# A down projection that streams 512 weight columns per stationary tile instead of 256

## The chip, the cores and the metric

The kernel runs on one core of a Trainium2 chip. The metric is the device time of one execution in microseconds (us); lower is better. The core has a matrix engine (PE in the profile, its weight loads PEld), a vector engine (DVE), a scalar engine (ACT), a general engine (POOL) and a queue engine (SP), which here issues weight loads. Each engine carries out its own instructions strictly in the order in which the program gives them, and waits at an instruction whose inputs or whose output buffer aren't free yet.

## The reference

One block of a diffusion model on 2048 tokens of width 1024: a gated linear attention branch and a pooling branch are mixed and added to the input, and then a mixture of experts follows. Only that last part is touched here. In it, 16 experts each choose the 256 tokens with the highest affinity to them (`top_k` over the tokens), and for each expert

```
xs = hs[idx]                                             # 256 tokens x 1024
a  = silu(xs @ w_gate_e) * (xs @ w_up_e)                 # 256 x 1024
y  = (a @ w_down_e) * wgt                                # 256 x 1024, the down projection
out = zeros.at[idx].add(y)
```

The result is scaled by a gate, added to the running activation, and every token row is normalized (`rms_norm` with `final_norm_g`). All arrays are float32.

## The kernel before, in words

**Three products for one.** To keep float32 accuracy at the matrix engine's fast rate, each operand is split into a high part in a shortened float32 format and a low part (the rest). `mm3` (L252 to L255) issues three matmuls for one product: high by high, high by low, low by high. Each has a stationary operand of 128x128 and a moving operand that streams past it.

**Weight units.** All weights come as units of 128x1024 float32 (512 KB), in one fixed list (`Units`, L60 to L108). For a unit, SP loads the raw tile `wraw` (3 buffers), ACT copies it to `whi` (L78), and DVE subtracts to get `wlo` (L85; POOL does it during the first expert, L1905). `whi` and `wlo` have 3 buffers each (the two 3s of L282): unit n+3 is written where unit n was, so its split on ACT can begin only when PE has finished with unit n.

**Items.** The order of all engines is written out by one Python loop. `Flow.item(n, mm)` (L156) does this for one piece of matrix work: it issues the matmuls of n units; then one step of the searches that are registered as `early`; then the eviction ("post") of the item before, with `flush_part`; then one step of each side generator; then the splits of as many units as the item gave back (`ahead`); and it keeps its own eviction for the next item. So DVE sees, for one item, first the splits behind that item and then, in the next item, its eviction.

**An expert** (loop at L1898) is 8 items `gate_up` (L1790; 2 units each: one tile of gate and one of up weights stationary, the 256 tokens moving, 48 matmuls of 256 columns into one bank `pA`), and then 4 items `down` (L1809; 2 units each). In a down item, `ah` and `al` (the activations, high and low) are stationary, 128 tokens at a time, and 256 columns of the down weights are moving: 2 token tiles x 8 contraction tiles x 3 = 48 matmuls. Both token tiles share one `pA` bank, 256 columns each. `LATE` (L45) gives the order: contraction tile 7, which needs the last gate_up item's activations, comes at the end. The eviction `fin` (L1823) multiplies each half by the token weights and the gate `gt2` on DVE (L1825) into `y`. Accumulator banks: `pA` has 3 buffers (L1591), `pG` 2 and `pT` 3. Between gate_up and down, and after down, `fl.flush()` issues the waiting eviction at once.

**Side work.** One step per item: `prep` (L1726) of the next expert (the one-hot tiles L1731, the gather of tokens, transposes), in the first expert also the search for the token choice of experts 2 to 15 (`topk_rest`, L1711, an `early` generator: a count on DVE, then the matmul L1719), and in the last six experts (`special`) more: after the eviction `fin_cols` (L1920) adds the old rows (L1922), `fin_late` (L1883) sums squares on ACT, `final_row` writes finished rows, and 16 generators `norm_row` (L1836), started 4 steps apart, normalize the rows of all tokens.

In the last expert's last down item (`split`) the two token tiles have a bank each, and the first tile is finished before the second begins.

Of the kernel before, what the change touches and what calls it, by code (L numbers as in the profile page):

```python
# [10 lines left out]
F32 = mybir.dt.float32  # L11
F32R = mybir.dt.float32r
BF = mybir.dt.bfloat16
I32 = mybir.dt.int32
AF = mybir.ActivationFunctionType
OP = mybir.AluOpType
# [5 lines left out]
L = 2048  # L22
LC = 256
KC = 8
T = 512
# [3 lines left out]
E = 16  # L29
# [15 lines left out]
LATE = ((0, range(4)), (1, range(4)), (0, range(4, 7)), (1, range(4, 7)), (0, (7,)), (1, (7,)))  # L45
# [184 lines left out]
def build(ctx, tc, A, out, dbg=None):  # L230
# [10 lines left out]
    def ps_a():  # L241
        return psum.tile([128, 512], F32, name="pA", bufs=2)
# [9 lines left out]
    def mm3(ps, lh, ll, rh, rl, first, last):  # L252
        PE.matmul(ps, lh, rh, start=first, stop=False)  # L253
        PE.matmul(ps, lh, rl, start=False, stop=False)  # L254
        PE.matmul(ps, ll, rh, start=False, stop=last)  # L255
# [27 lines left out]
    fl = Flow()  # L283
# [1522 lines left out]
            return fin  # L1806
        fl.item(2, mm)

    def down(j, ah, al, y, wt, cols, after, split):  # L1809
        cs = slice(j * 256, (j + 1) * 256)  # L1810

        def mm(w):
            ph = [ps_a(), ps_a()] if split else [ps_a()] * 2
            ph = [t[:, i * 256:(i + 1) * 256] for i, t in enumerate(ph)]
            for i, ks in ((0, range(KC)), (1, range(KC))) if split else LATE:
                for kc in ks:
                    wh, wl = w[kc // 4]
                    s = slice(kc % 4 * 256, (kc % 4 + 1) * 256)
                    ts = slice(i * 128, (i + 1) * 128)
                    mm3(ph[i], ah[:, kc, ts], al[:, kc, ts], wh[:, s], wl[:, s],  # L1820
                        kc == 0 and (i == 0 or split), kc == KC - 1 and (i == 1 or split))

            def fin():  # L1823
                for i in range(2):
                    V.scalar_tensor_tensor(y[i][:, cs], ph[i], wt[:, i:i + 1], gt2[:, cs],  # L1825
                                           op0=OP.mult, op1=OP.mult)
                    if cols:
                        cols(j, i)
                if after:
                    after()  # L1830
            return fin
        fl.item(2, mm)

    LASTK = 6

# [46 lines left out]

    def fin_late(j, i, e, y, acs, ss4, cs):  # L1883
        yield
        jf = mo.tile([128, L], BF, name="jf")[:, :256]
        S.activation(jf, y[i][:, cs], AF.Square, accum_out=ss4[:, i, j:j + 1])
        if e == E - 1:
            (V if j == 3 else G).tensor_mul(acs[i][:, cs], y[i][:, cs], fng[:, cs])

    res = {}  # L1890
    rest, keys = topk_rest(), keys_rest()
# [6 lines left out]
    for e in range(E):  # L1898
        special = e >= E - LASTK
        xh, xl, idx, wt = res.pop(e)  # L1900
        ah = mo.tile([128, 8, 256], F32R, name="ah", bufs=2)
        al = mo.tile([128, 8, 256], F32R, name="al", bufs=2)
        if e + 1 < E:
            fl.add(prep(e + 1, res))
        un.low2 = G if e == 0 else V  # L1905
        if e == 0:
            fl.early.append(rest)
            fl.add(chain(delay(AD), split_aff(slice(HEAD_N, E), E - HEAD_N)))
        acs = []
        if special:  # L1910
            fl.add(acc_gather(idx, acs))
        if e == E - LASTK:
            fl.add(chain(delay(2), staggered([lambda t=t: norm_row(t) for t in range(NSC)], 4)))
        for f in range(8):
            gate_up(f, xh, xl, ah, al)
        y = [mo.tile([128, D], F32, name=f"y{i}", bufs=2) for i in range(2)]

        ss4 = mo.tile([128, 2, 4], F32, name="ss4", bufs=2)

        def fin_cols(j, i, e=e, y=y, acs=acs, ss4=ss4, idx=idx):  # L1920
            cs = slice(j * 256, (j + 1) * 256)
            V.tensor_add(y[i][:, cs], y[i][:, cs], acs[i][:, cs])  # L1922
            if j < 2 or e < E - 1:
                fl.add(fin_late(j, i, e, y, acs, ss4, cs))
                return
            for _ in fin_late(j, i, e, y, acs, ss4, cs):
                pass
            if j == 3 and e == E - 1:
                for _ in final_row(i, e, y, acs, ss4, idx):
                    pass  # L1930

        def scat(e=e, y=y, idx=idx, special=special, ss4=ss4, acs=acs):
            if special and e < E - 1:
                fl.add(chain(delay(1), staggered([lambda i=i: final_row(i, e, y, acs, ss4, idx) for i in range(2)], 1)))
            elif not special:
                for i in range(2):
                    G.indirect_dma_start(out=x1_d[:, :],
                                         out_offset=bass.IndirectOffsetOnAxis(ap=idx[i][:, :1], axis=0),
                                         in_=y[i], in_offset=None, compute_op=OP.add)
        fl.flush()  # L1940
        for j in range(4):
            down(j, ah, al, y, wt, fin_cols if special else None, scat if j == 3 else None,
                 e == E - 1 and j == 3)
        fl.flush()
        if e == E - 1:
            fl.drain()
# [6 lines left out]
def host_inputs(inputs):  # L1953
    g = {k: np.ascontiguousarray(np.asarray(v)) for k, v in inputs.items()}
    c = np.ascontiguousarray
    w_in = g["w_in"][0]
    k0, v0, r0, q0, g0, p0, m0 = 0, 256, 768, 800, 1056, 1568, 2080

    def st_units(w):
        n = w.shape[1] // 128  # L1960
        return w.reshape(KC, 128, n, 128).transpose(2, 1, 0, 3).reshape(n, 128, 1024)

    def mv_units(w):
        n = w.shape[1] // 256
        return w.reshape(2, 4, 128, n, 256).transpose(3, 0, 2, 1, 4).reshape(2 * n, 128, 1024)

    rr = w_in[:, r0:r0 + 32]
    win = np.concatenate([st_units(np.concatenate([rr, rr, rr, rr], 1)), st_units(w_in[:, k0:k0 + 256]),
                          st_units(w_in[:, q0:q0 + 256]), mv_units(w_in[:, v0:v0 + 512]),
                          st_units(w_in[:, g0:g0 + 512]), st_units(w_in[:, p0:p0 + 512]),  # L1970
                          st_units(w_in[:, m0:m0 + 2048])])
    wdu = g["w_decay_up"][0].reshape(2, 16, H, 64)
    w32 = np.zeros((32, H, 128), np.float32)
    w32[0:16, :, 0:64] = wdu[0]
    w32[16:32, :, 64:128] = wdu[1]
    w32 = w32.reshape(32, 512)
    ab = g["ada_b"][0]
    vecs = np.concatenate([g["c"].reshape(8, 128), g["c_ctx"].reshape(8, 128), g["norm1_g"].reshape(8, 128),
                           ab[0:1024].reshape(8, 128), ab[1024:2048].reshape(8, 128),
                           g["b_decay"][0].reshape(2, H, 64).transpose(1, 0, 2).reshape(H, 128),  # L1980
                           g["pool_scale"].reshape(4, 128), g["gla_norm_g"].reshape(1, 128)])
    aw = g["ada_w"][0]
    ada1 = aw[:, :2048].reshape(KC, 128, 4, 512).transpose(2, 1, 0, 3)
    ada2 = aw[:, 2048:].reshape(4, 2, 128, 8, 512).transpose(3, 2, 0, 1, 4).reshape(8, 128, 4, 1024)

    def inv_counts(n):
        r = np.zeros((4, n), np.float32)
        pos = np.arange(n)
        for i, w in enumerate(WINDOWS):
            r[i] = 1.0 / (np.clip(pos + w // 2, 0, n) - np.clip(pos - w // 2, 0, n))  # L1990
        return r

    pj = np.concatenate([g["w_gla_proj"][0].reshape(4, 128, 8, 128), g["w_pool_proj"][0].reshape(4, 128, 8, 128)])
    pj = pj.transpose(2, 1, 0, 3).reshape(8, 128, 1024)
    wg = g["w_gate_e"][0].reshape(E, KC, 128, 8, 128).transpose(0, 3, 2, 1, 4).reshape(E, 8, 128, 1024)
    wu = g["w_up_e"][0].reshape(E, KC, 128, 8, 128).transpose(0, 3, 2, 1, 4).reshape(E, 8, 128, 1024)
    wdn = g["w_down_e"][0].reshape(E, 2, 4, 128, 4, 256).transpose(0, 4, 1, 3, 2, 5).reshape(E, 8, 128, 1024)
    return {
        "x": g["x"][0], "ctx": g["ctx"][0], "vecs": c(vecs), "ada1": c(ada1), "ada2": c(ada2),
        "ada_b2": c(ab[None, 2048:]), "win": c(win), "wdu": c(np.concatenate([w32] * 4)),  # L2000
        "pool_w": c(g["pool_w"][0].transpose(1, 0, 2)), "icc": inv_counts(64), "icr": inv_counts(32),
        "wpj": c(pj), "wout": c(mv_units(g["w_out"][0])),
        "w_router": c(g["w_router"][0].reshape(KC, 128, E).transpose(1, 0, 2)),
        "wg": c(wg), "wu": c(wu), "wdn": c(wdn),
        "norm2_g": g["norm2_g"].reshape(1, D), "final_norm_g": g["final_norm_g"].reshape(1, D),
    }
# [15 lines left out]
```

## Time and profile before

| | us |
|---|---|
| three runs of the kernel | 2653.22, 2662.35 (the median), 2670.72 |
| span of the profiled execution, first to last instruction | 2667.8 |
| mean granted TensorE clock in it | 0.972 |
| PE busy / DVE busy / ACT busy / POOL busy | 2517.5 / 1881.2 / 1252.5 / 659.1 |

The profiled execution's own time is its span, 2667.8 us; no other time is shown for it. It lies 5.45 us above the median of the runs and inside their spread. All stretches below are in us from the start of the span; the experts lie between 1476 and 2653. Busy times of PE are modelled (a matmul's record is longer than the distance to the next), so the distance between starts is what counts. In a timeline row the first number is the start, the second the duration, and the bracket at the end gives the idle time before it and what ended it.

### The profile page before, as it was taken

What the parts mean: (1) busy time and instruction counts of PE and PEld (TensorE: products, weight loads), DVE (VectorE), ACT (ScalarE), POOL (GpSimd) and SP (SyncE); (2) the same over time, 40 slices, a digit from 0 to 9 for tenths busy, and PEclk for the clock granted to TensorE, in tenths of its full rate; (3) what the DMA queues carried; (4) which work ended last, traced back from release to release, by engine and by line L of the source; (5) the groups of instructions that cost most, each with busy time, mean ns of one, the idle gap of its engine ahead of it and who ended that gap; (6) DMA issues with size and microseconds to landing.
All of it is one profiled execution on the core that took longest, in us unless ns stands there. A gap on an engine that the chain in (4) does not pass through costs nothing. (4 is left out here: it accounts for less than half of the span.)

```text
span 2667.8 us, 44973 instructions
## 1 busy us (share of the span) xinstructions
PE 2517.5 (94%) x17575; PEld 2295.5 (86%) x17575; DVE 1881.2 (71%) x3049; ACT 1252.5 (47%) x2128; POOL 659.1 (25%) x607
## 2 busy tenths in 40 slices
PE   7999999999998989999996899999999999999997
PEld 4878887887887768897886789999999999999997
DVE  6676668478368767767676866666666667778775
ACT  5454444344453345455553334444444445555553
POOL 0032157055225202131312550000000002323222
PEclk9999999999999989999997899999999999999999
DMA  7354356456435766656664356666666667787775
GB/s 259 125 188 164 137 186 220 144 174 213 161 112 170 251 225 221 222 185 225 199 210 139 127 174 212 215 204 209 212 207 214 211 209 251 262 276 258 252 248 183
DMA packets 202141, 537.00 MB, mean 201 GB/s; under 512 B 20871, under 2 KB 60216, under 8 KB 201928
## 3 DMA queue, kind: packets, MB, share of 16 engines
q1 hardware_dynamic: 141224, 408.77, 45.2%
q0 software_dynamic: 18592, 67.64, 8.8%
q10 hardware_dynamic: 42112, 57.72, 6.0%
q8 instruction: 138, 2.26, 0.3%
q14 instruction: 75, 0.61, 0.1%
HBM read 441.76 MB, written 92.29 MB: 200 GB/s over the span
## 5 line engine op out<-in xcount | busy, mean ns | idle before, releaser
L85 DVE TENSOR_TENSOR wlo<-wraw,whi 128x1024 fp32r<-128x1024 f32 x563 | 723.6, 1293 | 414.8 <-ACT whi L78 389.7
L78 ACT ACTIVATE whi<-wraw 128x1024 fp32r<-128x1024 f32 x595 | 623.8, 1055 | 619.7 <-PE pA L254 246.7
L255 PE MATMUL pA<-xh,wlo 128*128 128x256 f32 x2048 | 579.9, 283 | 17.3 <-DVE wlo L85 13.4
L253 PE MATMUL pA<-xh,whi 128*128 128x256 f32 x2048 | 582.1, 284 | 2.1 <-ACT whi L78 2.1
L254 PE MATMUL pA<-xl,whi 128*128 128x256 f32 x2048 | 577.4, 282 | 0.1
L255 PEld LDWEIGHTS pA<-xh,wlo 128*128 128x128 f32 x2048 | 388.0, 189 | 22.0 <-DVE wlo L85 17.4
L253 PEld LDWEIGHTS pA<-xh,whi 128*128 128x128 f32 x2048 | 388.0, 189 | 3.3 <-ACT whi L78 3.1
L254 PEld LDWEIGHTS pA<-xl,whi 128*128 128x128 f32 x2048 | 388.0, 189 | 0.4 <-DVE xl L1772 0.4
L253 PE MATMUL pA<-hh,whi 128*128 128x512 f32 (+1 forms) x912 | 366.4, 402 | 10.9 <-DVE kd L770 3.7
L255 PE MATMUL pA<-hh,wlo 128*128 128x512 f32 (+1 forms) x912 | 359.3, 394 | 0.4 <-DVE wlo L85 0.4
L254 PE MATMUL pA<-hl,whi 128*128 128x512 f32 (+1 forms) x912 | 359.1, 394 | 0.0
L253 PE MATMUL pA<-whi,ah 128*128 128x256 f32 x1024 | 290.3, 284 | 5.0 <-ACT ah L1804 5.0
L254 PE MATMUL pA<-wlo,ah 128*128 128x256 f32 x1024 | 287.4, 281 | 1.8 <-POOL wlo L85 1.1
L255 PE MATMUL pA<-whi,al 128*128 128x256 f32 x1024 | 287.8, 281 | 0.2 <-DVE al L1805 0.2
L253 PEld LDWEIGHTS pA<-hh,whi 128*128 128x128 f32 x912 | 175.4, 192 | 54.2 <-issue 8.9
L255 PEld LDWEIGHTS pA<-hh,wlo 128*128 128x128 f32 x912 | 174.9, 192 | 38.1 <-DVE wlo L85 0.7
L254 PEld LDWEIGHTS pA<-hl,whi 128*128 128x128 f32 x912 | 175.5, 192 | 34.3
L253 PEld LDWEIGHTS pA<-whi,ah 128*128 128x128 f32 x1024 | 193.7, 189 | 5.8 <-ACT ah L1804 5.8
L254 PEld LDWEIGHTS pA<-wlo,ah 128*128 128x128 f32 x1024 | 193.9, 189 | 2.6 <-POOL wlo L85 1.3
L255 PEld LDWEIGHTS pA<-whi,al 128*128 128x128 f32 x1024 | 193.7, 189 | 1.0 <-DVE al L1805 1.0
L1804 ACT ACTIVATE ah<-sg 128x256 fp32r<-128x256 f32 x128 | 53.5, 418 | 275.6 <-DVE sg L1803 275.6
L297 POOL TENSOR_TENSOR rs<-ms,neg_half 128x1 f32<-128x1 f32 (+2 forms) x70 | 54.5, 779 | 509.1 <-DVE ms L295 496.0
(438 smaller groups left out, 4787.7 us busy)
## 6 DMA issues: line engine op xcount, KB each, us to landing
wraw<-win SPq DMA_DIRECT2D x139, 512.0 KB
wraw<-wg SPq DMA_DIRECT2D x128, 512.0 KB
wraw<-wu SPq DMA_DIRECT2D x128, 512.0 KB
wraw<-wdn SPq DMA_DIRECT2D x128, 512.0 KB
wraw<-wout SPq DMA_DIRECT2D x40, 512.0 KB
ar<-ada SPq DMA_DIRECT2D x64, 256.0 KB
gate_d<-stg ACTq DMA_DIRECT2D x64, 256.0 KB
wraw<-wpj SPq DMA_DIRECT2D x32, 512.0 KB
```

Source lines behind the costliest of these rows:

```text
L78: self.nc.scalar.activation(hi, raw, AF.Copy)
L85: (self.low2 if self.s % 4 in LOWS else self.low).tensor_sub(lo, raw, hi.bitcast(F32))
L253: PE.matmul(ps, lh, rh, start=first, stop=False)
L254: PE.matmul(ps, lh, rl, start=False, stop=False)
L255: PE.matmul(ps, ll, rh, start=False, stop=last)
L297: G.tensor_tensor(r[:, :n], ms[:, :n], neg_half[:, :n], op=OP.pow)
L1804: S.activation(ah[:, f], sg, AF.Copy)
```

## The change

The columns of the down weights that one stationary tile meets grow from 256 to 512 (`T` is 512). An expert's down projection becomes 2 halves of 4 items, one unit per item. A unit now holds 2 contraction tiles x 512 columns (it held 4 x 256), and an item has 2 token tiles x 2 contraction tiles x 3 = 12 matmuls of 512 columns. Each token tile of a half has a whole `pA` bank, from the half's first item to its last; only the fourth item leaves an eviction, of 2 x 128x512. The number of `pA` buffers stays 3. Flags and indices of the side work follow: `fin_late` on 512 columns, two partial sums per row in place of four, and on the last expert's last half the multiply by `fng` on DVE. The `LATE` order and the `split` case are gone. The host lays the down weights out anew.

```diff
-    def down(j, ah, al, y, wt, cols, after, split):
-        cs = slice(j * 256, (j + 1) * 256)
-
-        def mm(w):
-            ph = [ps_a(), ps_a()] if split else [ps_a()] * 2
-            ph = [t[:, i * 256:(i + 1) * 256] for i, t in enumerate(ph)]
-            for i, ks in ((0, range(KC)), (1, range(KC))) if split else LATE:
-                for kc in ks:
-                    wh, wl = w[kc // 4]
-                    s = slice(kc % 4 * 256, (kc % 4 + 1) * 256)
+    def down(j, ah, al, y, wt, cols, after):
+        cs = slice(j * T, (j + 1) * T)
+        ph = [ps_a(), ps_a()]
+
+        def fin():
+            for i in range(2):
+                V.scalar_tensor_tensor(y[i][:, cs], ph[i], wt[:, i:i + 1], gt2[:, cs],
+                                       op0=OP.mult, op1=OP.mult)
+                if cols:
+                    cols(j, i)
+            if after:
+                after()
+
+        for q in range(4):
+            def mm(w, q=q):
+                wh, wl = w[0]
+                for i in range(2):
                     ts = slice(i * 128, (i + 1) * 128)
-                    mm3(ph[i], ah[:, kc, ts], al[:, kc, ts], wh[:, s], wl[:, s],
-                        kc == 0 and (i == 0 or split), kc == KC - 1 and (i == 1 or split))
...
-        fl.item(2, mm)
+                    for k2 in range(2):
+                        kc = 2 * q + k2
+                        s = slice(k2 * T, (k2 + 1) * T)
+                        mm3(ph[i], ah[:, kc, ts], al[:, kc, ts], wh[:, s], wl[:, s], kc == 0, kc == KC - 1)
+                return fin if q == 3 else lambda: None
+            fl.item(1, mm)
...
-        jf = mo.tile([128, L], BF, name="jf")[:, :256]
+        jf = mo.tile([128, L], BF, name="jf")[:, :T]
...
-            (V if j == 3 else G).tensor_mul(acs[i][:, cs], y[i][:, cs], fng[:, cs])
+            (V if j else G).tensor_mul(acs[i][:, cs], y[i][:, cs], fng[:, cs])
...
-        for j in range(4):
-            down(j, ah, al, y, wt, fin_cols if special else None, scat if j == 3 else None,
-                 e == E - 1 and j == 3)
+        for j in range(2):
+            down(j, ah, al, y, wt, fin_cols if special else None, scat if j else None)
```

## Rows read from the trace of the kernel before

**Rows 1.** The page, section 1: busy time, share of the span, instructions.

```profile
PE 2517.5 (94%) x17575; PEld 2295.5 (86%) x17575; DVE 1881.2 (71%) x3049; ACT 1252.5 (47%) x2128; POOL 659.1 (25%) x607
```

**Rows 2.** Windows: stretch, length, busy (records) by engine, clock, DMA share, GB/s.

```profile
1921.00:1991.00 70.00, 70.00 (x625) 69.96 (x624) 47.96 (x82) 32.13 (x44) 5.53 (x4) 1.00 0.67 211
2347.00:2423.00 76.00, 71.82 (x624) 70.42 (x623) 59.32 (x97) 41.53 (x69) 21.48 (x16) 1.00 0.75 260
2499.00:2579.00 80.00, 73.36 (x623) 71.68 (x621) 60.59 (x98) 42.20 (x70) 20.08 (x16) 0.98 0.74 257
```

**Rows 3.** Timeline of PE, a down projection: start, duration, instruction, tiles, shape.

```profile
1905.01 0.28 PE L255 MATMUL pA<-whi,al 128*128 128x256 f32 x1
...
1921.46 0.27 PE L255 MATMUL pA<-whi,al 128*128 128x256 f32 x1
```

**Rows 4.** Timeline of all engines, the end of one down item.

```profile
1915.86 0.28 PE L255 MATMUL pA<-whi,al 128*128 128x256 f32 x1
...
1916.17 1.06 ACT L78 ACTIVATE whi<-wraw 128x1024 fp32r<-128x1024 f32 x1 [1.74 <-PE pA L255]
...
1917.27 1.22 DVE L85 TENSOR_TENSOR wlo<-wraw,whi 128x1024 fp32r<-128x1024 f32 x1 [1.58 <-ACT whi L78]
...
1918.41 0.87 DVE L1825 SCALAR_TENSOR_TENSOR y<-pA,wt,gt 128x256 f32<-128x256 f32 x2
```

**Rows 5.** Timeline of PE, two earlier stretches of 512-column matmuls.

```profile
898.25 0.39 PE L253 MATMUL pA<-hh,whi 128*128 128x512 f32 x1
...
918.46 0.39 PE L255 MATMUL pA<-hh,wlo 128*128 128x512 f32 x1
...
980.22 0.40 PE L253 MATMUL pA<-ogh,whi 128*128 128x512 f32 x1
...
1005.18 0.40 PE L255 MATMUL pA<-ogh,wlo 128*128 128x512 f32 x1
```

**Rows 6.** DVE lines with 512 columns from PSUM: count, duration in ns min/median/max.

```profile
L1019 DVE SCALAR_TENSOR_TENSOR mxl<-pT,vt,mxh x16: 736/742/752, 942.0 to 1307.9; 128x512 fp32r<-128x512 f32 x16
...
L1482 DVE TENSOR_TENSOR ga<-ga,pA x32: 627/680/771, 985.2 to 1368.9; 128x512 f32<-128x512 f32 x32
```

**Rows 7.** Timeline of PE, the first down item of the first expert.

```profile
1541.41 0.28 PE L253 MATMUL pA<-whi,ah 128*128 128x256 f32 x1
...
1548.45 0.39 PE L1719 MATMUL pG<-mv,blk 128*128 128x8 f32 x2 [2.26 <-DVE mv L1718]
```

**Rows 8.** Waits from 1570 to 1600: who, for whom, total us, times, longest.

```profile
PE pA L255 <- DVE wlo L85: 1.8, 2, 1.3
```

**Rows 9.** Timeline of DVE and PE, the second gate_up item of expert 11.

```profile
2277.34 3.80 DVE L1731 TENSOR_SCALAR oh<-iob,slot 128x256 bf16<-128x256 bf16 x8
...
2282.32 0.39 PE L255 MATMUL pA<-xh,wlo 128*128 128x256 f32 x1 [0.72 <-DVE wlo L85]
```

**Rows 10.** Waits of PE from 2190 to 2668.

```profile
PE pA L255 <- DVE wlo L85: 11.6, 13, 2.3
PE pA L253 <- ACT ah L1804: 5.0, 4, 2.1
```

**Rows 11.** Timeline of DVE, PE and POOL, the end of the program.

```profile
2650.00 0.48 DVE L1825 SCALAR_TENSOR_TENSOR y<-pA,wt,gt 128x256 f32<-128x256 f32 x1 [0.78 <-PE pA L255]
...
2652.51 0.28 PE L255 MATMUL pA<-whi,al 128*128 128x256 f32 x1
...
2654.35 1.02 POOL L1881 DMA_INDIRECT out<-ac,ix  x1 [1.48 <-ACT ac L1880]
```

**Rows 12.** Timeline of PE: two long idle gaps of expert 14.

```profile
2510.60 0.39 PE L255 MATMUL pA<-xh,wlo 128*128 128x256 f32 x1 [2.33 <-DVE wlo L85]
...
2560.19 0.39 PE L253 MATMUL pA<-whi,ah 128*128 128x256 f32 x1 [2.10 <-ACT ah L1804]
```

**Rows 13.** Windows behind those two gaps (columns as in rows 2).

```profile
2510.60:2514.00 3.40, 3.40 (x28) 3.40 (x29) 2.77 (x8) 1.47 (x6) 0.14 (x1) 1.00 0.97 317
...
2560.49:2563.88 3.39, 3.39 (x18) 3.24 (x17) 3.14 (x4) 2.61 (x4) 2.91 (x2) 0.50 0.28 111
```

More of the change, by code (lines that the diff above doesn't have):

```diff
@@ L1807, in gate_up @@
         fl.item(2, mm)
-    def down(j, ah, al, y, wt, cols, after, split):
-        cs = slice(j * 256, (j + 1) * 256)
-        def mm(w):
-            ph = [ps_a(), ps_a()] if split else [ps_a()] * 2
-            ph = [t[:, i * 256:(i + 1) * 256] for i, t in enumerate(ph)]
-            for i, ks in ((0, range(KC)), (1, range(KC))) if split else LATE:
-                for kc in ks:
-                    wh, wl = w[kc // 4]
-                    s = slice(kc % 4 * 256, (kc % 4 + 1) * 256)
-                    ts = slice(i * 128, (i + 1) * 128)
-                    mm3(ph[i], ah[:, kc, ts], al[:, kc, ts], wh[:, s], wl[:, s],
-                        kc == 0 and (i == 0 or split), kc == KC - 1 and (i == 1 or split))
[L1823 to L1831, printed above, removed]
-        fl.item(2, mm)
+    def down(j, ah, al, y, wt, cols, after):
[13 more added lines that the diff above has]
+                for i in range(2):
+                    ts = slice(i * 128, (i + 1) * 128)
+                    for k2 in range(2):
[4 more added lines that the diff above has]
+            fl.item(1, mm)
     LASTK = 6
@@ L1916, in build @@
         y = [mo.tile([128, D], F32, name=f"y{i}", bufs=2) for i in range(2)]
-        ss4 = mo.tile([128, 2, 4], F32, name="ss4", bufs=2)
+        ss4 = mo.tile([128, 2, 2], F32, name="ss4", bufs=2)
         def fin_cols(j, i, e=e, y=y, acs=acs, ss4=ss4, idx=idx):
-            cs = slice(j * 256, (j + 1) * 256)
+            cs = slice(j * T, (j + 1) * T)
             V.tensor_add(y[i][:, cs], y[i][:, cs], acs[i][:, cs])
-            if j < 2 or e < E - 1:
+            if j == 0 or e < E - 1:
                 fl.add(fin_late(j, i, e, y, acs, ss4, cs))
@@ L1927, in fin_cols @@
                 pass
-            if j == 3 and e == E - 1:
+            if e == E - 1:
                 for _ in final_row(i, e, y, acs, ss4, idx):
@@ L1996, in host_inputs @@
     wu = g["w_up_e"][0].reshape(E, KC, 128, 8, 128).transpose(0, 3, 2, 1, 4).reshape(E, 8, 128, 1024)
-    wdn = g["w_down_e"][0].reshape(E, 2, 4, 128, 4, 256).transpose(0, 4, 1, 3, 2, 5).reshape(E, 8, 128, 1024)
+    wdn = g["w_down_e"][0].reshape(E, 4, 2, 128, 2, T).transpose(0, 4, 1, 3, 2, 5).reshape(E, 8, 128, 1024)
     return {
```

## Prediction, before the changed kernel ran

> **What bounds the kernel now.** I read the page's busy times first: PE leads with 94%, DVE has 71%, ACT 47% [rows 1]. A modelled busy time says only that PE is nearly always in use, so I looked at the stretches of single experts next [rows 2]. Expert 6 (1921 to 1991) is fully covered by PE at the full clock, with DVE busy 48 of 70 us: PE alone bounds it. Experts 11 to 14 take 75 to 80 us; there PE stands still for some us while DVE is busy for 59 to 61 us, and the last ends on late splits. So the matrix engine's spacing counts in most of the part, and DVE's order in the rest. Third, the spacing: in a down projection 141 steps from one matmul to the next take 16.45 us, 116.7 ns each [rows 3]. Fourth, the cycle of one unit [rows 4]: the last matmul of a unit starts at 1915.86; ACT's split of the unit three later begins at 1916.17, 0.03 us after that matmul's record ends, because it writes the same buffer; DVE's low half starts 1.10 us after it, and DVE's next instruction, the eviction of the down item, 1.14 us after that. This eviction is late by 2.55 us every time. Today nobody minds: the next down items go to the two other banks, and the bank is wanted again two items (11.2 us) on.
>
> **The change, part by part.**
>
> *Columns.* 3072 matmuls of 256 columns become 1536 of 512. Dense stretches of 512 columns run at 20.21 us for 89 steps, 227.1 ns, and in another stage at 24.96 us for 107 steps, 233.3 ns [rows 5]. Two old steps are 233.4 ns. So a pair gains between 0 and 6.3 ns; I take 6.3, since that stretch, like the experts, has operands made by the same split and is as dense: 1536 x 6.3 ns = 9.7 us gained. Bounds: 0 and 9.7. By the Trainium skill (TensorE: Matmul & The Clock Gate, section Back-to-back issue gap) the distance at full clock is N/2.4 ns plus 2.5 ns, 109 and 216 ns; by that, as an estimate, a pair gains 2.5 ns and all of them 3.9 us, and the sum below would be 5.8 us higher. This trace has 116.7 and 227.1 ns, more than the page says at either width, so I go by the rows.
>
> *The bank.* A half holds two banks for its four items. The second half therefore needs four banks while the first half's two wait for eviction, and there are three. Its first token tile takes the free one; its second token tile needs the bank of the first half's first tile. Count from s, the start of the first half's last matmul. That record ends at s+0.39 [rows 5]; ACT's split follows at +0.03, DVE's low half 1.10 later, the eviction 1.14 later [rows 4], because the splits behind an item stand ahead of the item's eviction on DVE. The eviction's first instruction has 512 columns from PSUM and takes 0.74 us [rows 6]; with 0.03 to wake PE this gives s+3.43. PE can do six matmuls meanwhile (the free bank) and arrives at s+7x0.227 = s+1.59. It waits 1.84 us. Behind the waiting matmul stand all others of PE, and so all later splits; since buffers come free only when PE is done with a unit, nothing runs ahead and nothing is made up later. 16 experts x 1.84 = 29.4 us. No row before shows such a wait; below it is bounded by 0 (eviction ahead of the split), above by 2.5 us each (another DVE instruction such as one of rows 6 in front), 40 us.
>
> *Expert 0.* The last count of its search ends in a matmul that stands behind the first down item and waits for DVE until 1548.45 [rows 7]. That item is now one unit instead of two; the second unit's 24 x 116.7 ns = 2.8 us used to run before this wait and now come after it: 2.8 us lost. In exchange the search ends before expert 1 begins, and expert 1's two waits of 1.8 us [rows 8] should go: 1.8 gained.
>
> *Evictions in the last six experts.* Behind the last down item DVE has two evictions and two additions, then the one-hot tiles, then the low halves that the second gate_up item needs; expert 11 waits 0.72 us there [rows 9], expert 14 2.33 us [rows 12]. Each of the four instructions grows from 0.48 [rows 11] to 0.74 us: 1.04 us later in each of experts 11 to 14, which have no slack: 4.2 us lost. The others have slack: expert 6 shows none of these waits.
>
> *Wait for `ah`.* 5.0 us in four waits [rows 10], as contraction tile 7 comes 42 matmuls into the projection. It now comes in the fourth unit, 8.2 us in. But the low half of that unit stands behind the same late DVE chain, so I trade it for an equal wait: 0, with 5.0 gained as the other bound.
>
> *Side work.* An expert has 16 steps instead of 12. The 16 row generators, 4 steps apart, span 4 experts instead of 5.3, so expert 14 is relieved and 10 to 13 get a row more each. Expert 14 costs 4 us more than 12 [rows 2]; I take 2 gained, bounds 4 either way. SP's queue keeps one load per split, in the same order; its row loads sit at the same steps of gate_up. POOL keeps its scatters; two multiplies of the last expert go to DVE, which is idle by then.
>
> *The end.* The first token tile's eviction starts at 2650.00 and its row scatter at 2654.35, 4.35 us on and 1.84 after the start of the last matmul [rows 11]; the second scatter follows it. Now that tile is finished only six matmuls (1.36 us) before the end, so its eviction starts 0.94 us before the last matmul does, and the scatter 3.41 us after: 1.6 us lost.
>
> *Clock.* An idle gap of 2.10 us was followed by 3.4 us at half clock, one of 2.33 us was not [rows 12, 13]. Half clock costs half of 3.4 us, 1.7. The gap of expert 0 and two of the grown gaps in experts 12 to 14 should add three such drops: 5.1 us, bounds 0 and 10. The new bank waits are idle for 1.84 less the 0.17 us by which the record outlasts the step, 1.67 us, shorter than either gap.
>
> **Sum:** -9.7 + 29.4 + 2.8 - 1.8 + 4.2 + 0 - 2 + 1.6 + 5.1 = +29.6 us on the span of 2667.8, which I take to be the execution's time. The runs' median is 2662.35, 5.45 lower; the same difference on it gives 2692.
>
> **Rivals.**
>
> *The bank wait is not there* (not slower). Place: the second half's first item. For it: the first tile is complete 1.36 us before the item ends, so an eviction that DVE did at once would be over in time. It decides from the point where the eviction ends by s+1.59 instead of s+3.43. Against: DVE works in order, and the low half ahead of it starts only at s+1.52 and no sooner, since its split waits for PE [rows 4]. Without 29.4 the sum is +0.2: 2663 us, no change. Chance 0.12.
>
> *The clock falls at every bank wait* (slower still). For: 1.67 us of idle is not far from the 2.10 that did it; a slightly later eviction closes the distance. Against: 2.33 us once did nothing. Half of 16 drops add 13.6 us, all add 27: 2706 to 2719. Chance 0.13.
>
> *The bank wait is partly absorbed,* because experts 11 to 15 wait for weights anyway and loads catch up during it: five of the sixteen waits and the grown gaps vanish, 9.2 and 4.2 us: 2679. For: DMA is busy 74 to 75% there [rows 2]. Against: loads, too, are released by PE's progress. Chance 0.07.
>
> *My forecast,* chance 0.68, has 2692 with its terms' bounds giving 2680 to 2705.
>
> **The numbers.** Predicted 2692. The range from 2658 to 2722 takes in all cases but the tails of each; main case alone 2680 to 2705. What a measurement of this kernel can tell from no change is about 1%, 27 us, so the border is 2689. Of the main case about 0.62 lies above it (0.42); the clock rival lies wholly above (0.13): slower 0.55. The rest of the main case (0.26), the absorbed wait (0.07) and most of the first rival (0.10) are within 1%: 0.43. Faster, 0.02: it would need no bank wait and the full gains besides.
>
> **What would show it.** In each expert PE should have one gap of about 1.7 us idle, six matmuls into the second half, ended by DVE's eviction (L1825 before); steps of 227 ns within a half; a longer first wait for the search matmul in expert 0, and no waits early in expert 1; gaps in the second gate_up item of experts 11 to 14 about 1 us longer. If the gap is absent, or ends by something else, my main term is wrong; if steps are 233 ns, there is no gain from columns; if the granted clock falls in experts 1 to 10, the clock rival holds.

## The result, and the profile after

| | before | after |
|---|---|---|
| median of four runs each, us | 2665.74 | 2722.66 |
| lowest to highest, us | 2653.22 to 2670.72 | 2715.64 to 2730.17 |
| span of the profiled execution, us | 2667.8 | 2713.9 |
| mean granted TensorE clock in it | 0.972 | 0.967 |

The changed kernel is slower: the ratio is 1.0226, interval 1.02 to 1.0252. Between the medians lie 56.9 us, between the two profiled executions 46.1 us, because after's profiled execution is the fastest of its four (2715.64) and before's is above its median. What follows places the 46.1 us; the other 10.8 us are seen in no trace.

Busy times hardly tell where the time went. Page of the changed kernel, section 1 (busy us, share of the span, instructions), and one line of section 5 (busy, mean ns | idle before, what ended it):

```profile
PE 2521.0 (93%) x16039; PEld 2222.6 (82%) x16039; DVE 1871.5 (69%) x2961; ACT 1246.7 (46%) x2080; POOL 650.5 (24%) x603
...
L253 PE MATMUL pA<-whi,ah 128*128 128x512 f32 x512 | 211.5, 413 | 41.6 <-DVE y L1815 41.6
```

Against [rows 1], 1536 PE instructions went and PE's busy time did not: it is 3.5 us higher. The second line is new: 41.6 us of idle time in front of the down matmuls, ended by the eviction (L1815, which was L1825).

**By place.** I cut both traces at the start of the first gate_up matmul of each expert and of the last matmul. The forecast column holds the prediction's terms, sorted by the same places.

| us | before | after | difference | forecast |
|---|---|---|---|---|
| ahead of expert 0 | 1476.85 | 1474.56 | -2.3 | 0 |
| expert 0 | 91.0 | 98.3 | +7.3 | +5.7 |
| experts 1 to 9 | 634.6 | 649.0 | +14.4 | +9.3 |
| experts 10 to 15, to the last matmul | 450.0 | 474.7 | +24.7 | +13.0 |
| last matmul to the end | 15.25 | 17.29 | +2.0 | +1.6 |

The stretch ahead of expert 0 is untouched by the change; it took 1466.9 to 1476.8 us in the kernels traced here, so 2.3 us are within its spread. Experts 1 to 9 are the plain case. Timeline of the changed kernel, all engines, where the first half of expert 5's down projection ends and the second begins (start, duration, engine, line, instruction):

```profile
1918.84 1.23 DVE L85 TENSOR_TENSOR wlo<-wraw,whi 128x1024 fp32r<-128x1024 f32 x1 [1.57 <-ACT whi L78]
...
1920.50 1.06 ACT L78 ACTIVATE whi<-wraw 128x1024 fp32r<-128x1024 f32 x1 [1.69 <-PE pA L255]
...
1921.47 0.40 PE L255 MATMUL pA<-whi,al 128*128 128x512 f32 x1
1921.59 1.22 DVE L85 TENSOR_TENSOR wlo<-wraw,whi 128x1024 fp32r<-128x1024 f32 x1 [1.53 <-ACT whi L78]
1922.74 1.40 DVE L1815 SCALAR_TENSOR_TENSOR y<-pA,wt,gt 128x512 f32<-128x512 f32 x2
...
1923.54 0.50 PE L253 MATMUL pA<-whi,ah 128*128 128x512 f32 x1 [1.67 <-DVE y L1815]
```

The order is that of [rows 4]: split on ACT, low half on DVE, then the eviction. But now PE wants the bank that the eviction empties. PE starts the second half at 1920.30, its sixth matmul at 1921.47, is then out of free banks, and goes on at 1923.54, when the first eviction is over: 2.07 us from start to start, 1.67 us idle. The same wait stands in each of experts 1 to 9. Waits of PE there, changed kernel, 1570 to 2190 (who, for whom: total, times, longest):

```profile
PE pA L253 <- DVE y L1815: 13.4, 8, 1.7
```

Expert 1's two waits of [rows 8] are gone, as is every other wait of PE. Expert 9's bank wait lies beyond 2190.

The columns gave nothing. Timeline of PE, the same down projection:

```profile
1912.14 0.39 PE L254 MATMUL pA<-wlo,ah 128*128 128x512 f32 x1
...
1920.77 0.39 PE L255 MATMUL pA<-whi,al 128*128 128x512 f32 x1
```

That is 37 steps in 8.63 us, 233.2 ns each, twice the 116.7 ns of [rows 3]: the slower of the two spacings of [rows 5].

In the last six experts the picture is another. Windows of the changed kernel: expert 6, expert 12 (columns as in [rows 2]):

```profile
1933.40:2005.60 72.20, 70.53 (x530) 65.67 (x529) 47.59 (x77) 32.00 (x44) 6.72 (x4) 1.00 0.67 205
2384.50:2469.40 84.90, 74.20 (x529) 67.61 (x528) 60.46 (x91) 42.91 (x64) 23.39 (x18) 0.96 0.73 248
```

Waits of PE, changed kernel, from 2190 to the end, and then waits of ACT in that stretch:

```profile
PE pA L253 <- DVE y L1815: 24.9, 7, 6.5
PE pA L255 <- DVE wlo L85: 10.5, 10, 3.0
PE pA L254 <- DVE wlo L85: 5.3, 3, 2.7
```

```profile
ACT whi L78 <- DMA out<-y,ix: 18.7, 3, 6.5
...
ACT jf L1844 <- DMA xf<-x_d: 14.4, 5, 4.4
```

PE waits up to 6.5 us for an eviction, not 1.67. The `ah` waits of [rows 10] are gone, and waits for low halves in the down projection (L254) stand in their place. ACT has two waits that the same view of before does not have at all: for a DMA into `out`, and for a row load. One of them, in expert 12, changed kernel, all engines:

```profile
2445.34 1.15 ACT L1850 ACTIVATE xf<-xf,rs 128x1024 f32<-128x1024 f32 x1 [0.77 <-POOL xf L1848]
2445.48 1.81 POOL L1881 DMA_INDIRECT out<-y,ix  x1 [0.18 <-issue]
...
2452.55 0.34 ACTq L1852 DMA_DIRECT2D out<-xf  x1
2452.99 2.00 ACT L78 ACTIVATE whi<-wraw 128x1024 fp32r<-128x1024 f32 x2 [6.51 <-DMA out<-y,ix]
2454.08 2.36 DVE L85 TENSOR_TENSOR wlo<-wraw,whi 128x1024 fp32r<-128x1024 f32 x2 [5.96 <-ACT whi L78]
...
2456.36 0.74 DVE L1815 SCALAR_TENSOR_TENSOR y<-pA,wt,gt 128x512 f32<-128x512 f32 x1
...
2457.16 0.80 PE L253 MATMUL pA<-whi,ah 128*128 128x512 f32 x1 [6.48 <-DVE y L1815]
```

POOL issues the scatter of expert 11's rows into `out` at 2445.48. ACT's next instruction in order is the write of a normalized row into `out` (`norm_row`, L1852), which must come after that scatter. It leaves at 2452.55. The two splits behind it on ACT start at 2452.99, their low halves on DVE at 2454.08, and the eviction, behind these, at 2456.36. PE has stood 6.48 us. The wait carries the eviction's name, and its cause is three engines away.

Windows of the changed kernel, stretches behind long gaps (the third column from the right is the granted clock; 0.50 is the level of 1.2 GHz):

```profile
1562.97:1566.37 3.40, 3.40 (x15) 2.76 (x16) 1.53 (x3) 1.06 (x1) 0.50 (x1) 1.00 0.50 154
1923.54:1926.94 3.40, 3.40 (x15) 2.77 (x16) 1.22 (x2) 1.06 (x1) 0.00 (x0) 1.00 0.49 163
...
2370.30:2377.10 6.80, 4.58 (x11) 3.62 (x12) 4.80 (x8) 2.77 (x6) 2.37 (x2) 0.50 0.52 169
2455.60:2462.40 6.80, 5.24 (x12) 4.13 (x13) 4.80 (x7) 2.73 (x7) 2.91 (x2) 0.50 0.50 157
2537.50:2544.30 6.80, 3.56 (x8) 2.81 (x9) 5.13 (x7) 2.77 (x5) 1.35 (x2) 0.50 0.64 219
```

Behind a bank wait of 1.67 us the clock stays at 1.00. In the last three windows, which begin within the grown gaps of experts 11 to 13 (4.45, 6.48 and 6.18 us), it is 0.50. From the start of the down projection of expert 0 to the last matmul, 37.5 us run at half clock, against 6.8 us before.

Two smaller places: the search matmul in expert 0, and POOL at the end, changed kernel.

```profile
1546.57 0.60 PE L1719 MATMUL pG<-mv,blk 128*128 128x8 f32 x2 [7.30 <-DVE mv L1718]
```

```profile
2700.51 1.02 POOL L1881 DMA_INDIRECT out<-ac,ix  x1 [1.48 <-ACT ac L1880]
```

Against [rows 7] the idle time before the search's last matmul rises from 2.26 to 7.30 us. The first row scatter is issued 3.88 us after the start of the last matmul (2696.63); in [rows 11] it was 1.84, and 3.41 was forecast.

### The profile page after: what moved, and what is told of

It reads as the page before. It is cut to its first block, busy times and chain, and to the rows that moved or that the text cites. A ratio compares the mean times of both kernels' runs of the same rounds, so it can differ in the third digit from the quotient of the medians.

```text
span 2713.9 us, 41755 instructions
## 1 busy us (share of the span) xinstructions
PE 2521.0 (93%) x16039; PEld 2222.6 (82%) x16039; DVE 1871.5 (69%) x2961; ACT 1246.7 (46%) x2080; POOL 650.5 (24%) x603
## 5 line engine op out<-in xcount | busy, mean ns | idle before, releaser
L254 PE MATMUL pA<-xl,whi 128*128 128x256 f32 x2048 | 578.2, 282 | 0.1
L254 PEld LDWEIGHTS pA<-xl,whi 128*128 128x128 f32 x2048 | 388.7, 190 | 1.1 <-DVE xl L1772 0.4
L254 PE MATMUL pA<-hl,whi 128*128 128x512 f32 (+1 forms) x912 | 357.9, 392 | 0.0
L253 PE MATMUL pA<-whi,ah 128*128 128x512 f32 x512 | 211.5, 413 | 41.6 <-DVE y L1815 41.6
L254 PE MATMUL pA<-wlo,ah 128*128 128x512 f32 x512 | 206.5, 403 | 5.3 <-DVE wlo L85 5.3
L255 PE MATMUL pA<-whi,al 128*128 128x512 f32 x512 | 205.7, 402 | 0.0
L254 PEld LDWEIGHTS pA<-hl,whi 128*128 128x128 f32 x912 | 174.7, 192 | 34.1
L1937 POOL DMA_INDIRECT x_d<-y,ix x20 | 37.8, 1892 | 520.3 <-DVE y L1815 456.5
L253 PEld LDWEIGHTS pA<-whi,ah 128*128 128x128 f32 x512 | 98.7, 193 | 70.9 <-DVE y L1815 48.6
L253 PE MATMUL pA<-whi,yh 128*128 128x256 f32 x512 | 148.5, 290 | 2.4 <-ACT yh L1487 1.4
```

The costliest lines, as they stand in the source:

```text
L1937: G.indirect_dma_start(out=x1_d[:, :], out_offset=bass.IndirectOffsetOnAxis(ap=idx[i][:, :1], axis=0), in_=y[i], in_offset=None, compute_o ...
```

## The experiments

Two theories. **A:** the loss in the plain experts is a question of order: the eviction stands on DVE behind the low half, and three banks leave PE no other. Rival: it is the wider eviction or the wider matmul itself. **B:** the loss of the last six experts is not the bank but the pace of the side work. The down projection gives the generators a step every 2.8 us (12 matmuls of 233 ns) in place of every 5.6, and row writes, scatters and row loads that were far enough apart now catch each other up on ACT. Rival: the bank wait, longer there because DVE is late.

Per expert, in us of each kernel's profiled execution (cut as above; "last six" is experts 10 to 15):

| kernel | expert 0 | experts 1 to 9 | last six |
|---|---|---|---|
| before | 91.0 | 634.6 | 450.0 |
| after | 98.3 | 649.0 | 474.7 |
| eviction first | 94.8 | 631.7 | 472.9 |
| pairs | 94.0 | 648.9 | 474.0 |
| pairs, eviction first | 94.3 | 631.8 | 455.3 |
| singles of 256 columns | 95.0 | 632.1 | 474.1 |
| four banks | 96.6 | 631.6 | 468.1 |
| eviction first, row write later | 97.2 | 631.7 | 460.2 |
| eviction first, rows spread | 96.6 | 632.1 | 454.6 |
| before, split first | 91.2 | 634.6 | 449.2 |

**The eviction first.** After, with the eviction of the first half issued within its own item, ahead of the splits:

```diff
-            fl.item(1, mm)
+            fl.item(1, mm, now=j == 0 and q == 3)
```

> The changed kernel with one edit: the eviction of an expert's first half is issued ahead of the splits behind its fourth item, not behind them. The banks and the single units stay. Theory A (the bank wait: the eviction is late because a split stands before it on DVE): the idle gap of 1.67 us that ends by the eviction vanishes from all experts, 16 x 1.84 = 29 us, and in experts 10 to 13 what the gap had grown by, 13 us: 2722 - 42 = 2680 us, not above 2693. Theory B (the side steps, twice as dense in the down projection, put a row write on ACT behind a scatter's landing, and so cost the time): only the plain experts gain, experts 10 to 13 keep their excess over before, as a wait for late splits: 2693 to 2705 us.

2691.06 us, ratio to before 1.0115 (1.0095 to 1.0135). Timeline of this kernel, around the same place in a plain expert:

```profile
1902.46 1.23 DVE L85 TENSOR_TENSOR wlo<-wraw,whi 128x1024 fp32r<-128x1024 f32 x1 [1.57 <-ACT whi L78]
...
1903.60 1.40 DVE L1815 SCALAR_TENSOR_TENSOR y<-pA,wt,gt 128x512 f32<-128x512 f32 x2
...
1904.12 1.06 ACT L78 ACTIVATE whi<-wraw 128x1024 fp32r<-128x1024 f32 x1 [1.69 <-PE pA L255]
...
1905.21 1.22 DVE L85 TENSOR_TENSOR wlo<-wraw,whi 128x1024 fp32r<-128x1024 f32 x1 [0.21 <-ACT whi L78]
```

Windows of this kernel, expert 6 and expert 12:

```profile
1915.10:1985.30 70.20, 70.20 (x530) 65.72 (x529) 47.72 (x77) 32.15 (x44) 5.64 (x4) 1.00 0.67 210
2358.90:2444.40 85.50, 74.94 (x530) 68.81 (x529) 61.52 (x91) 43.06 (x64) 24.33 (x18) 0.94 0.71 248
```

The eviction now runs 0.52 us before ACT's split even starts, and PE is covered for the whole of expert 6: 70.2 us, the length before. Theory A holds for experts 1 to 9. Without the bank wait their 70.2 us also show that 512 columns save nothing. The last six keep 472.9 us, and there the bank wait is not gone. Waits of PE, this kernel, from 2190 to the end:

```profile
PE pA L253 <- DVE y L1815: 15.9, 4, 5.3
```

These four waits are those of experts 10 to 13. In expert 12 ACT stands behind a row write until 2429.47; the low half of the split that follows is made at 2430.56, and only behind that, at 2431.70, comes the eviction. Issued early, it is still late, because a split of an earlier item stands ahead of it. So this run, whose total falls into what theory A expected, does not tell the two causes apart in the last six.

**Pairs.** After, with two units per item, as before the change (4 items per expert; columns, banks and eviction as after):

```diff
-        for q in range(4):
+        for q in range(2):
...
-            fl.item(1, mm)
+            fl.item(2, mm)
```

> The changed kernel with its units consumed in pairs again: 512 columns, two banks per half, 2 items of 24 matmuls per half, so 12 side steps per expert as before. Theory A: the bank wait of 1.84 us stays in all 16 experts, 29 us over the kernel before, 2695 us, and experts 10 to 13 fall back to before plus the wait. Theory B: the larger part of the loss lies in experts 0 and 10 to 13 and goes away: the ACT queue no longer stands at a row write for 6 us; with the bank wait still there 2690 to 2697 us. If neither holds, it stays at 2722 us. Expert 0 should lose its 7 us excess under both.

2712.51 us, 1.0195 (1.0175 to 1.0215). The plain experts wait just as long (waits of PE, this kernel, 1580 to 2190):

```profile
PE pA L253 <- DVE y L1815: 13.0, 8, 1.7
```

ACT has neither of the two new waits in the last six experts, and they still take 474.0 us. Waits of PE, this kernel, from 2190 to the end (one of the seven is expert 9's):

```profile
PE pA L253 <- DVE y L1815: 18.4, 7, 3.6
```

So the pace of the side work is not the only thing that can cost the last six their 24 us: with the old pace, the bank wait does most of it. Its six waits would cost 11 us by their size in a plain expert; they are 1.92 to 3.59 us long, 16.8 us in all. This run had been expected at 2690 to 2697 us under either theory, with the whole excess of expert 0 gone; it is 15 us slower than that, and expert 0 keeps 3.0 us.

**Pairs and the eviction first.** Both edits.

```diff
+            fl.item(2, mm, now=j == 0 and q == 1)
```

> Pairs and the early eviction together: 512 columns and two banks per half are all that is left of the change. If the two theories together hold the whole loss, this is the kernel before plus the longer end (1.6 us) and the later second item of experts 11 to 14 (4 us): 2666 to 2672 us, within noise of before. If 512 columns gain anything, it shows here: 9.7 us at 227 ns a step, 0 at 233 ns as the trace of the changed kernel has it. Any remainder above 2680 us would be a third cause.

2673.15 us, 1.0046 (1.0031 to 1.0061). Waits of PE, this kernel, from 2190 to the end; no wait for an eviction is among them:

```profile
PE pA L255 <- DVE wlo L85: 13.1, 11, 3.6
PE pA L254 <- DVE wlo L85: 8.5, 11, 2.1
```

The last six fall to 455.3 us, 18.8 below the pairs alone. With the bank wait and the new pace both gone 5.2 us are left. By the medians 12 us are left over before. In the profiled executions, from expert 0 on, 7.8 are seen: expert 0 with 3.35, the last six with 5.24, the end with 2.05, less 2.85 in experts 1 to 9. That is what 512 columns cost with no wait for the bank and the old pace; nothing in it is a gain but expert 1's two waits.

**Singles of 256 columns.** Before, with one unit per item in the down projection and nothing else: theory B by itself, without wide columns and without a shortage of banks: a group of two items holds one bank of the three. (The last item of the last expert stays as it was.)

```diff
-        fl.item(2, mm)
+        if split:
+            fl.item(2, mm)
+            return
...
+        for n in range(2):
+            def mm1(w, n=n):
...
+                for i, ks in LATE[:2] if n == 0 else LATE[2:]:
...
+                return fin1 if n else lambda: None
+            fl.item(1, mm1)
```

> The kernel before with its down units consumed singly and nothing else: 256 columns, one bank for both token tiles, 8 items of 24 matmuls per expert, so 16 side steps; the last item of the last expert as before. Theory A: no bank is short, so plain experts stay at 70.2 us, and the time is that of before, 2666 us, but for expert 0 (about 3 to 5 us more for its search). Theory B: experts 0 and 10 to 13 lose as in the changed kernel, less what the free banks absorb (two units, 5.5 us, of each 6 us stop on ACT): 2672 to 2690 us.

2687.42 us, 1.0097 (1.0072 to 1.0122). Plain experts 70.2 us, last six 474.1. PE waits for no eviction in this kernel. Waits of ACT, this kernel, from 2190 to the end (L1869 is its line for L1844):

```profile
ACT jf L1869 <- DMA xf<-x_d: 16.8, 5, 4.2
...
ACT whi L78 <- DMA out<-y,ix: 14.3, 2, 7.5
```

Both stops of ACT are there, in a kernel with before's columns and before's evictions. Theory B holds: consuming units singly costs the last six 24.1 us, and nothing elsewhere but 4.0 us in expert 0.

**Four banks.** After, with a fourth bank for `pA`, taken from the transposes:

```diff
-        return psum.tile([128, 512], F32, name="pA", bufs=3)
+        return psum.tile([128, 512], F32, name="pA", bufs=4)
...
-        return psum.tile([128, 512], F32, name="pT", bufs=3)
+        return psum.tile([128, 512], F32, name="pT", bufs=2)
...
-            ps = [ps_t(), ps_t(), ps_t(), ps_a()]
+            ps = [ps_t(), ps_t(), ps_a(), ps_a()]
```

> The changed kernel with four pA banks instead of three (one taken from pT; expert 0's first transposes use two pA banks). Order and single units stay. If the wait is for a bank, the idle gap in the second half's first item vanishes from experts 1 to 9 although the eviction is as late as before: 70.2 us each instead of 72.1, and the run is like the one with the early eviction, 2691 us against 2661 of before. If the order on DVE by itself made PE late (late splits), the gap stays: 2721 us.

2688.78 us, 1.0074 (1.0047 to 1.0102). Window of this kernel, expert 6:

```profile
1921.40:1991.60 70.20, 70.20 (x530) 65.71 (x529) 47.60 (x77) 32.05 (x44) 6.15 (x4) 1.00 0.66 210
```

With a fourth bank the late eviction bothers nobody, again 70.2 us. The order and the number of banks are two remedies for the same wait, so theory A's two halves (late, and no other bank) are both shown. By the Trainium skill (Perfetto Trace Analysis, section Identifying Performance Opportunities), the same gap repeating on the engine that should be saturated can mean that PSUM ran out for the next tile; this trace agrees, with 1.67 us in nine experts, gone with one bank more. The last six keep 468.1 us and both of ACT's stops, and PE waits for no eviction there either (waits of ACT, this kernel, from 2190 to the end):

```profile
ACT jf L1844 <- DMA xf<-x_d: 19.5, 6, 4.2
...
ACT whi L78 <- DMA out<-y,ix: 12.8, 2, 6.5
```

This is the run that shows the pace alone at 512 columns: 18.1 us in the last six with no bank wait.

**The row write later.** The eviction first, and `norm_row` writes its row two steps later, past the scatter that it met:

```diff
         fl.later(lambda: S.activation(x, x, AF.Copy, scale=r[:, 0:1]))
-        yield
+        yield from delay(3)
```

> The early eviction with single units, and the row generators' write on ACT issued two steps later, when the scatter it must follow has landed. If ACT's three stops of 5.5 us at the row write are what dense steps cost in the last six experts, these fall from 473 us towards the 456 of the pairs with the early eviction, and the run from 2691 to about 2675 us (3 us of it remain in expert 0). If the stops at the square (ACT waiting for a row load, 4.3 us each, four or five times) are as much of it, only part returns: 2680 to 2686 us. If it is the density of DMA traffic and not these waits, nothing moves: 2691 us.

2677.39 us, 1.0048 (1.0033 to 1.0064), against 1.0115 with the early eviction alone. The wait of ACT for `out` is gone, and with it the four waits of PE for an eviction that the early eviction alone had left; the one for the row load is larger (this kernel, from 2190 to the end):

```profile
ACT jf L1844 <- DMA xf<-x_d: 26.9, 8, 6.4
```

The last six fall by 12.7 us, to 460.2. So that stop alone cost about half of their loss.

**The rows spread.** The same, and the square of a row comes five steps after its load instead of one (`yield` behind the load becomes `yield from delay(5)`). This moves row writes past an expert's final write of the same row, so some rows of the output hold the plain normalized row; the work is the same.

> As the last one, and the square of a row four steps later too, so that the row's load has landed when ACT comes to it. If the two ACT waits are the whole of what dense side steps cost, the last six experts are at 456 us or less and the run at 2670 to 2676 us, level with the pairs; if a remainder stays (DMA traffic, weights loaded late), between that and 2691 us.

2674.47 us, 1.0028 (1.0012 to 1.0044). Waits of ACT, this kernel, from 2190 to the end:

```profile
ACT jf L1886 <- DMA out<-y,ix: 15.8, 3, 5.5
```

The row load's wait is gone, but the write into `out` waits again, at a later step, now ahead of another instruction (L1886, `fin_late`'s square). The last six take 454.6 us, 5.7 less than in the kernel ahead; the interval of the total overlaps that kernel's, so the gain of this second step is not shown by the times. Of the excess of 24.7 us in the last six, 4.5 are left.

**A try on before.** Since DVE's order decides, the first gate_up item of an expert, whose splits stand behind the one-hot tiles in the last experts [rows 9], got its next split within the item, ahead of these:

```diff
-        fl.item(2, mm)
+        fl.item(2, mm, mid=(lambda: un.ahead(1)) if f == 0 else None)
```

> The kernel before with one edit that these runs point to: in the first gate_up item of each expert one split is issued ahead of the side step, so that on DVE the low half that the second item needs stands before the eight one-hot instructions. The four waits there in experts 11 to 14 (0.72, 1.25, 1.75 and 2.33 us) should shrink or go: up to 6 us, 2655 against 2661 us, a ratio of 0.998, if nothing else is late behind them; if the one-hot tiles or the weights' loads then decide, no difference.

2659.72 us, 0.9988 (0.9972 to 1.0004): no difference. The last six take 449.2 us against 450.0. Waits of PE, this kernel, 2190 to the end:

```profile
PE pA L255 <- DVE wlo L85: 10.7, 14, 1.8
PE pA L253 <- ACT ah L1804: 4.4, 4, 1.6
PE pA L253 <- ACT whi L78: 1.8, 5, 0.5
PE pA L254 <- DVE wlo L85: 1.2, 5, 0.4
```

Before, the same view has these two beside those of [rows 10]:

```profile
PE pA L253 <- ACT whi L78: 2.1, 5, 0.5
PE pA L254 <- DVE wlo L85: 0.7, 3, 0.2
```

The sum of the four is 18.1 us against 19.4 before, in 28 waits against 25, the longest 1.8 us against 2.3. The four waits that the edit aimed at, 6.05 us, are gone; 5.29 us of waits stand one item later in the same experts. The waits were moved, not removed. No version was found that is faster than before.

## Why the prediction was right or wrong

The direction and the bank wait were right, the size was not: 29.6 us were forecast, and the profiled executions differ by 46.1. Two terms of the sum failed, the columns and the side work, and the bank wait was sized for plain experts only. Point by point:

- **The bank wait: right in the plain experts, too small in the last six.** 1.67 us idle and 1.84 us lost in each plain expert, six matmuls into the second half, ended by the eviction, for the reason given (the low half ahead of it on DVE). That the 1.84 is met to the digit is in part luck: PE arrives 0.04 us later than forecast, its steps being 233 ns, and goes on 0.04 us later too. In the plain experts a fourth bank or an earlier eviction takes the wait away, and the clock did not fall at it, so that rival is out. In the last six experts the wait was forecast at 11.0 us and took 23.2 us of idle time in the changed kernel. The absorbed wait is out as well: all of experts 11 to 15 have the wait, at 1.67 to 6.48 us.
- **The columns: this step failed.** The prediction says "so a pair gains between 0 and 6.3 ns; I take 6.3". A pair gained 0: 233.2 ns a step in the dense stretch, and 70.2 us for a plain expert of 512 columns without the bank wait, as for one of 256. This term of the sum was mis-sized by all of its 9.7 us; 5.4 of them belong to experts 1 to 9, which took 5.1 more than forecast (14.4 against 9.3). The two rows of [rows 5] contradicted each other, and the choice between them rested on a likeness ("operands made by the same split") that was no reason.
- **Side work: this step failed too, and it was the larger.** The prediction says "I take 2 gained, bounds 4 either way", from a count of how many row generators fall on which expert. That count was right: expert 14 got 5.6 us shorter and expert 15 3.1, as the rows end sooner. What was not asked is what the steps of two generators do to each other when they come twice as fast. In experts 10 to 13, 33.5 us more are spent than before, against 7.4 for four bank waits of plain size. In place of 2 us gained, the pace alone costs the last six 18.1 us with four banks and 24.1 in the singles of 256 columns, net of that relief.
- **Bank and pace don't add.** With 512 columns the last six take 455.3 us with neither (pairs, eviction first), 468.1 with the pace alone (four banks), 474.0 with the bank wait alone (pairs) and 474.7 with both. So the 11 us forecast there as the bank's are in the measured loss, but not on top of the pace's. The bank wait alone costs 18.8 us there instead of 11, and its six waits are 16.8 us of it. Why they are longer than in a plain expert was not tested.
- **Clock: too small.** The forecast was "three such drops", 5.1 us, with a bound of 10. There were 30.7 us more at half clock than before, which is up to 15 us of lost time if PE was wanted throughout; it was not, as its busy share in the three stretches shown at half clock is 52% to 77%. The stops of ACT, which were missed, are only part of the cause: the singles of 256 columns have 44.4 us at half clock, but pairs, without these stops, still have 23.9, with the eviction first or not, against 6.8 before.
- **Expert 0:** 7.3 us against 5.7. The search matmul still waits for the same DVE chain (from the one ahead of it to itself 10.4 us before, 10.8 after), and 2.8 us of matmuls came behind it, as forecast. In addition its bank wait was 3.3 us of idle time instead of 1.67 (here POOL makes the low halves, and the eviction stands on DVE behind side work that ends at 1562.26), and 6.8 us ran at half clock instead of 3.4.
- **Expert 1:** its two waits went, as forecast. **`ah`:** its waits were traded for waits for low halves, as forecast. **Evictions:** forecast were 1.04 us more in each second gate_up item of experts 11 to 14; measured were 0.72, 1.25, 1.75 and 2.33 us of wait before and 2.99, 1.35, 1.34 and 1.96 after, 1.6 us more in all and not 4.2. **The end:** 2.0 against 1.6.

The places sum up to the error: 5.1 in experts 1 to 9, 1.6 in expert 0, 11.7 in the last six, 0.4 at the end, less 2.3 ahead of the experts, 16.5 us. The medians add 10.8, which no trace places.

## What to carry to other kernels

An item is also a clock: whoever changes how many items a stage has changes the pace of everything that steps once per item, and must check which of those steps wait for each other's transfers, on the engine that makes the operands above all. Where a bank is held over several items, count banks held plus banks waiting for eviction, and look at what stands ahead of the eviction on its engine; one bank more or the eviction issued first were equal remedies in the plain experts (70.2 us with either), but an early eviction helps only if nothing late stands ahead of it: in the last six experts it left 15.9 us of waits, one bank more left none. A wait is named after its last link: behind the 6.5 us of PE for an eviction stood a row write on ACT's queue.

## What the runs showed of the hardware

- **Time per column is the same at 256 and 512.** Dense steps in the down projection take 116.7 and 233.2 ns, 0.456 ns per column at both widths, with a weight load of 128x128 for each matmul in both. Why one earlier stage has 227.1 ns at 512 columns [rows 5] stays open. The rule of the Trainium skill that the prediction weighed (TensorE: Matmul & The Clock Gate, section Back-to-back issue gap: N/2.4 ns plus 2.5 ns, which the section gives for an isolated matmul) would have a pair gain 2.5 ns; the measurement has no gain.
- **The length of a gap does not decide alone whether the clock falls.** 3.31 us in expert 0 was followed by a granted clock of 1.00 (2.4 GHz), as was 1.67 us in nine experts; within the 6.48 us of expert 12 it fell to 0.50 (1.2 GHz), within the 2.79 us of expert 10 too, and 2.10 us in expert 14 before was followed by 0.50 [rows 12, 13].
- **A transfer issued from ACT stops ACT's computing while it waits.** In expert 12 the row write stood for 6.06 us (2446.49 to 2452.55) behind a scatter into the same output, and both splits behind it with it, though none of them needs the row.
